# Interleaving the chunks of a seven-product FFN: the next chunk's first products among the last products of the chunk before, and three empty slots ahead of its third product

## The chip, the cores and the metric

One NeuronCore of a Trainium2 chip runs the whole program. The metric is device time in microseconds (us) of one execution. The kernel before was timed in three runs: 2363.18, 2362.95 and 2358.63 us, median 2362.95 us. One more execution, of 2361.89 us, was taken with the profiler; its instructions span 2360.2 us, and every duration in this document comes from it.

## The reference, cut to what matters

One layer on 256 tokens and 2048 channels, in float32:

```python
x = LN(ALPHA*x + 0.5*swiglu(x, ffn1_w1, ffn1_w3, ffn1_w2))
x = LN(ALPHA*x + mixer(x))          # mLSTM and stick-breaking branches
x = LN(ALPHA*x + 0.5*swiglu(x, ffn2_w1, ffn2_w3, ffn2_w2))
x = x + sigmoid(x @ w_ple_gate) * (p @ w_ple_proj)
swiglu(x, w1, w3, w2) = (silu(x @ w1) * (x @ w3)) @ w2   # 2048 -> 5632 -> 2048
```

The change touches only the two FFNs (the two swiglu calls). Their weights are 2048 x 5632 twice and 5632 x 2048, and each weight element is read at least once per FFN for just 256 tokens.

## The kernel before, in words

**Matmuls.** Each float32 operand is split in two float32r parts, hi and lo, and a product is made of three matmuls: hi x hi, hi x lo, lo x hi (L1046, L1047, L1048). The stationary operand is a 128 x 128 tile of the transposed activations `actT`, the moving one 128 x 512 of a weight. A **unit** is six such matmuls (256 rows of contraction) into one PSUM bank. The program is a Python list of units, and TensorE (PE) executes them in the order of this list.

**Weights.** A unit's weight is a `raw` tile of 256 x 512 (512 KB), loaded by a DMA issued on SP (L968). It is split by ScalarE (ACT, the cast at L995: hi) and VectorE (DVE, the subtraction at L999: lo). Splits are emitted in the order in which the units first use them, and the loop at L1008 to L1011 keeps seven of them alive, so that in an FFN a split is emitted seven or eight units ahead of its use. Loads run ahead of the splits: at most 12 raw tiles may be held in an FFN (`RAW_FFN`), and fewer where the 44 buffers of the `page` pool run short (L962, L963). ACT and DVE each execute in program order, so an instruction emitted behind a split waits until that split's raw tile has landed.

**FFN.** The 5632 hidden columns are 11 chunks of 512. Chunks 0 and 5 are computed plainly (`up`). The other nine (1, 2, 3, 4, 6, 7, 8, 9, 10) use `up7`: tokens in two halves, contraction in two halves, and the pair w1, w3 as two column blocks make a 2 x 2 block product that takes seven products instead of eight (function `seven`). Each product of a chunk is four units (a, b, c, d: one for each 512 rows of contraction). They go by the numbers in the code:

- product 1 uses a quarter t of w1; product 5 uses t plus a quarter of w3; product 6 uses that sum plus another quarter of w3; product 4 uses it plus the quarter b21 of w1, and product 2 b21 alone;
- products 7 and 3 use b12 + b22 and b22, loaded again from w3.

The two sums for products 5 and 6 are made in place by **growing** the raw tile: as soon as product 1's split has read t, a DMA issued on GpSimd (POOL, L328) adds the quarter of w3 to t in SBUF, and after product 5's split a second one adds the next. There are four tiles, so eight such DMAs for each chunk, 144 in all. The sums for products 4 and 7 are DVE additions (L333).

Products 1 and 2 accumulate in a bank X, 5 and 4 in a bank E. After 5d (the last unit of product 5) ACT copies E to SBUF (`e`, L443), and DVE writes X - e to a fixed bank B (L437); this write is called the **seed** below. Product 6 accumulates onto it, so 6a, product 6's first unit, cannot start before the seed. After 6d ACT copies B to the bank W (L448), onto which product 7 accumulates; product 3 goes on in B. After product 7 and 3 the two halves of the hidden chunk are finished (silu, multiplications at L459 and L470), transposed on PE (L264), copied by ACT (L266) and subtracted by DVE (L272) to make `actT` tiles for the down product.

**Order.** `weave` (L155) lays the list of the nine chunks' units (the side list) evenly among the other units of the FFN (the main list: chunks 0 and 5, and the down products `down(c)`, which need chunk c's hidden tiles). An entry `None` of the side list is an empty slot: it takes a place in the weaving and emits nothing. Before, the side list is the nine chunks one after another, each of 28 units and two empty slots between product 5 and product 6:

1a 1b 1c 1d | 5a 5b 5c 5d | two empty slots | 6a 6b 6c 6d | 2a 2b 4a 2c 4b 2d 4c 4d | 7a 3a 7b 3b 7c 3c 7d 3d

The 270 entries are woven among 184 main units. Between 5d and 6a then stand two main units (three in chunk 7), between 1a and 5a, counted from one to the other, six or seven units, and between 5a and 6a eight (nine in chunk 7).

Of the kernel before, what the change touches and what calls it, by code (L numbers as in the profile page):

```python
# [154 lines left out]
def weave(main, side):  # L155

    n = sum(isinstance(u, Unit) for u in main)
    out, at, seen = [], 0, 0
    for u in main:
        out.append(u)  # L160
        if isinstance(u, Unit):
            seen += 1
            while at < len(side) and at * n < seen * len(side):
                if side[at] is not None:
                    out.append(side[at])
                at += 1
    return out


def flat(pairs):  # L170
    return [u for p in pairs for u in p]
# [7 lines left out]
def kernel(  # L179
# [7 lines left out]
    x, out = x[0], out[0]  # L187
# [124 lines left out]
    def seven(wa, wb, rows, col0, cols, act, done):  # L312

        n = rows // (4 * P)
        banks = {k: {} for k in "XEBW"}

        def unit(m, i, tile, src, half, sub, bank, first):
            u = Unit(tile, half, banks[bank], src, i, sub, first and i == 0, i == n - 1,
                     lambda ps, t, m=m: done(m, banks))
            u.onto = not first  # L320
            return u
# [15 lines left out]
        one, five, six, two, four, rest = [], [], [], [], [], []  # L337
        for i in range(n):
# [8 lines left out]
            b12, b22 = quarter(wb, i, 0), quarter(wb, i, 2)  # L347
            rest.append(unit(7, i, Weight(b12, [b12, b22], [b12], plus(b12, b22)), act.forms, 1, 0, "W", False))
            rest.append(unit(3, i, Weight(b22, [], [b22]), act.forms, 1, 2, "B", False))
        lead = two[:1]  # L350
        for i in range(n):
            lead += two[i + 1:i + 2] + four[i:i + 1]
        return one + five + [None, None] + six + lead + rest

    program = []

# [53 lines left out]
    def ffn(w1, w3, w2, act, norm, skew=True, ahead=()):  # L410
        n = FF // COL
# [21 lines left out]
        def up7(c):  # L433
# [35 lines left out]
            def late(w):  # L469
# [4 lines left out]
                yield  # L474

            return seven(w1, w3, D, c * COL, COL, act, done)

        def down(*chunks):
            pairs = []
            for g in range(D // COL):  # L480
                def add(ps, t, g=g):
                    xs = xres[t][:, g * COL:(g + 1) * COL]
                    nc.vector.scalar_tensor_tensor(out=xs, in0=ps, scalar=0.5, in1=xs,  # L483
                                                   op0=ALU.mult, op1=ALU.add)
                    if n - 1 in chunks:
                        norm.chunk(t, g)
                pairs += group(w2, [c * COL + r for c in chunks for r in (0, 2 * P)], g * COL, COL, hT, add)
            return pairs
# [2 lines left out]
        program.extend((skewed(gate[0][:SKEW]) if skew else flat(gate[0][:SKEW])) + flat(gate[0][SKEW:]))  # L491
        rest, tail = down(8, 9), down(10)
        main = flat(hidden[0] + gate[1] + down(0) + down(1) + down(2) + down(3) + down(4) + hidden[1] + down(6) + down(5, 7))
        program.extend(main[:8] + weave(main[8:] + flat(rest[:8]), [u for c in (1, 2, 3, 4, 6, 7, 8, 9, 10) for u in up7(c)]))
        program.append(norm.load)
        program.extend(ahead)
        program.extend(flat(rest[8:]) + flat(tail[:-SKEW]) + skewed(tail[-SKEW:]))
# [12 lines left out]
    x1T = ActT(act_tile)  # L510
    norm1 = Norm(ln1_g[0], ln1_b[0], x1T, None)
    ffn(ffn1_w1[0], ffn1_w3[0], ffn1_w2[0], xT, norm1, skew=False, ahead=[lambda: mixer_setup()])


# [361 lines left out]
    x3T = ActT(act_tile)  # L876
    norm3 = Norm(ln3_g[0], ln3_b[0], x3T, None)
    ffn(ffn2_w1[0], ffn2_w3[0], ffn2_w2[0], x2T, norm3)


# [147 lines left out]
    for u in program:  # L1028
# [6 lines left out]
        j = u.tile.index  # L1035
# [50 lines left out]
```

## Time and profile before

| | |
|---|---|
| median of three runs | 2362.95 us (2358.63 to 2363.18) |
| the profiled execution | 2361.89 us, span 2360.2 us |
| first FFN, its woven part from chunk 2's product 6 to chunk 10's | 153.8 to 676.5 us |
| mixer and the plain products around it | about 771 to 1481 us |
| second FFN, the same woven part | 1626.3 to 2154.1 us |
| PE, PE weight loads, DVE, ACT, POOL busy in the whole span | 2236.6, 1839.7, 1734.9, 1260.3, 221.4 us |

How to read the views: PE is the engine that has the most work, so what counts is where PE waits and where its matmuls start further apart than they could. The view of the waits says who waited for whom (total us, times, longest). The timeline lists instructions in order of time (start, duration, engine, line, what it writes and reads, in brackets the idle time before it and what ended it); "x2" marks two instructions merged in one row. The view by windows gives busy time of each engine in a stretch, the granted PE clock as a share of full speed, the share of time in which the 16 DMA engines were busy, and the rate in GB/s.

### The profile page before, as it was taken

To read this page: it belongs to the slowest core of one execution; us is meant where nothing else is said; L and a number is where in the kernel's file an instruction comes from. 1 tells how busy PE (TensorE), PEld (TensorE's weight loads), DVE (VectorE), ACT (ScalarE), POOL (GpSimd) and SP (SyncE) were. 2 spreads that over 40 slices of the span, in tenths; PEclk is the share of its full clock that TensorE was granted. 3 is DMA by queue.
4 is the path that set the end of the run, shared out by engine and by line. 5 is a ranking of instruction groups with operands and counts; after the bars stand their busy time and mean duration, and the time that the engine had idled before them with its cause. 6 is when DMAs were issued, how large, how long until landed. Compare 5 with 4: busy or idle time off the path is not lost. (4 is left out here: it accounts for less than half of the span.)

```text
span 2360.2 us, 27588 instructions
## 1 busy us (share of the span) xinstructions
PE 2236.6 (95%) x10017; PEld 1839.7 (78%) x10017; DVE 1734.9 (74%) x1884; ACT 1260.3 (53%) x1471; POOL 221.4 (9%) x191
## 2 busy tenths in 40 slices
PE   9898998999989999999999999998899899998999
PEld 7676877788768888888888888777687777876878
DVE  6877898898878765654445556887789788886874
ACT  5555565665555455544643443555555556555542
POOL 3011101111000000100100000301111011100000
PEclk9899999999999999999999999999999999999999
DMA  9778988889785565665566577577897898978643
GB/s 322 212 193 244 268 245 235 232 221 290 223 262 209 172 187 160 177 182 158 161 188 196 182 228 248 147 226 199 226 271 242 233 240 204 289 221 254 242 149 108
DMA packets 267209, 510.22 MB, mean 216 GB/s; under 512 B 16000, under 2 KB 25024, under 8 KB 267072
## 3 DMA queue, kind: packets, MB, share of 16 engines
q1 hardware_dynamic: 227904, 432.95, 55.8%
q0 software_dynamic: 39168, 75.51, 18.0%
q8 instruction: 78, 1.28, 0.2%
q14 instruction: 59, 0.48, 0.1%
HBM read 506.30 MB, written 2.10 MB: 215 GB/s over the span
## 5 line engine op out<-in xcount | busy, mean ns | idle before, releaser
L999 DVE TENSOR_TENSOR split<-raw,split 128x1024 fp32r<-128x1024 f32 (+1 forms) x1037 | 1219.1, 1207 | 429.4 <-ACT split L995 406.7
L995 ACT CAST split<-raw 128x1024 fp32r<-128x1024 f32 (+1 forms) x1037 | 1042.2, 1037 | 659.2 <-DMA raw<-in_ffn_w_dram 250.2
L1046 PE MATMUL mm<-split,actT 128*128 128x512 f32 (+2 forms) x2704 | 1060.3, 392 | 15.2 <-ACT actT L258 12.8
L1048 PE MATMUL mm<-split,actT 128*128 128x512 f32 (+2 forms) x2704 | 1047.8, 387 | 8.8 <-DVE actT L272 7.5
L1047 PE MATMUL mm<-split,actT 128*128 128x512 f32 (+2 forms) x2704 | 1047.3, 387 | 4.7 <-DVE split L999 4.7
L1046 PEld LDWEIGHTS mm<-split,actT 128*128 128x128 f32 x2704 | 513.1, 190 | 118.7 <-ACT actT L258 15.0
L1048 PEld LDWEIGHTS mm<-split,actT 128*128 128x128 f32 x2704 | 512.4, 190 | 116.4 <-DVE actT L272 10.1
L1047 PEld LDWEIGHTS mm<-split,actT 128*128 128x128 f32 x2704 | 513.4, 190 | 106.0 <-DVE split L999 7.6
L328 POOL DMA_DIRECT2D raw<-in_ffn_w_dram x144 | 173.9, 1217 | 1105.4 <-DMA raw<-in_ffn_w_dram 589.7
L1046 PE MATMUL seeded<-split,actT 128*128 128x512 f32 x432 | 180.6, 418 | 84.2 <-DVE seeded L437 84.2
L1047 PE MATMUL seeded<-split,actT 128*128 128x512 f32 x432 | 177.6, 411 | 0.0
L1048 PE MATMUL seeded<-split,actT 128*128 128x512 f32 x432 | 176.6, 409 | 0.0
L333 DVE TENSOR_TENSOR raw<-raw 128x1024 f32<-128x1024 f32 x144 | 175.5, 1219 | 0.2 <-issue 0.2
L1046 PEld LDWEIGHTS seeded<-split,actT 128*128 128x128 f32 x432 | 86.5, 200 | 109.0 <-DVE seeded L437 91.0
L483 DVE SCALAR_TENSOR_TENSOR xres<-mm,xres 128x512 f32<-128x512 f32 x144 | 98.3, 685 | 7.0 <-PE mm L1048 7.0
L1048 PEld LDWEIGHTS seeded<-split,actT 128*128 128x128 f32 x432 | 86.9, 201 | 19.3
L1047 PEld LDWEIGHTS seeded<-split,actT 128*128 128x128 f32 x432 | 87.0, 201 | 17.8
L266 ACT CAST actT<-ms 128x512 fp32r<-128x512 f32 x84 | 48.9, 587 | 81.8 <-PE ms L264 79.3
L272 DVE TENSOR_TENSOR actT<-ms,actT 128x512 fp32r<-128x512 f32 x84 | 57.2, 685 | 22.2 <-ACT big L271 10.8
L407 POOL TENSOR_SCALAR xres<-xres 128x512 f32<-128x512 f32 x16 | 27.1, 1787 | 320.5 <-DVE xres L390 300.5
L236 ACT ACTIVATE temp<-mm 128x512 f32<-128x512 f32 (+1 forms) x36 | 20.5, 570 | 44.9 <-PE mm L1048 44.9
L236 ACT ACTIVATE big<-mm 128x512 f32<-128x512 f32 x20 | 12.0, 599 | 55.8 <-PE mm L1048 55.8
(124 smaller groups left out, 639.4 us busy)
## 6 DMA issues: line engine op xcount, KB each, us to landing
raw<-in_ffn_w_dram SPq DMA_DIRECT2D x527, 512.0 KB, 6.2
raw<-in_w_in_dram SPq DMA_DIRECT2D x168, 512.0 KB, 3.7
raw<-in_ffn_w_dram POOLq DMA_DIRECT2D x144, 512.0 KB, 9.6
raw<-in_w_out_dram SPq DMA_DIRECT2D x32, 512.0 KB, 5.1
raw<-in_w_ple_gate_dram SPq DMA_DIRECT2D x24, 512.0 KB, 4.9
raw<-in_w_up_m_dram SPq DMA_DIRECT2D x16, 512.0 KB, 3.7
raw<-in_w_up_sb_dram SPq DMA_DIRECT2D x16, 512.0 KB, 3.9
raw<-in_w_ple_gate_dram SPq DMA_DIRECT2D x16, 256.0 KB, 4.4
```

Source lines behind the costliest of these rows:

```text
L236: nc.scalar.activation(out, in_, func, **kw)
L266: nc.scalar.copy(dst[:, 0], ps[:])
L272: nc.vector.tensor_tensor(out=dst[:, 1], in0=ps[:], in1=dst[:, 0], op=ALU.subtract)
L328: nc.gpsimd.dma_start(out=raw.tile[:, :, :cols], in_=src.src, accum_op=ALU.add)
L333: nc.vector.tensor_tensor(out=a.tile[:, :, :cols], in0=a.tile[:, :, :cols], in1=b.tile[:, :, :cols], op=ALU.add)
L407: nc.gpsimd.tensor_scalar(out=xs, in0=xs, scalar1=ALPHA, scalar2=None, op0=ALU.mult)
L483: nc.vector.scalar_tensor_tensor(out=xs, in0=ps, scalar=0.5, in1=xs, op0=ALU.mult, op1=ALU.add)
L995: nc.scalar.copy(hi[:, ks], r[:, ks])
L999: nc.vector.tensor_tensor(out=lo[:, ks], in0=r[:, ks], in1=hi[:, ks], op=ALU.subtract)
L1046: nc.tensor.matmul(ps, hi, w[0][:, k, :u.cols], start=first, stop=False, skip_group_check=u.onto)
L1047: nc.tensor.matmul(ps, hi, w[1][:, k, :u.cols], start=False, stop=False, skip_group_check=u.onto)
L1048: nc.tensor.matmul(ps, lo, w[0][:, k, :u.cols], start=False, stop=last, skip_group_check=u.onto)
```

## The change

`seven` no longer joins its parts; a new function `chained` makes the side list of all nine chunks.

```diff
         rest.append(unit(3, i, Weight(b22, [], [b22]), act.forms, 1, 2, "B", False))
-        lead = two[:1]
-        for i in range(n):
-            lead += two[i + 1:i + 2] + four[i:i + 1]
-        return one + five + [None, None] + six + lead + rest
+        return one, five, six, two, four, rest
+
+    def chained(parts):
+
+        out = list(parts[0][0])
+        for j, (_, five, six, two, four, rest) in enumerate(parts):
+            ahead = list(parts[j + 1][0]) if j + 1 < len(parts) else []
+            n = len(five)
+            out += five + [None] * 3 + six + two[:1]
+            for i in range(n):
+                out += two[i + 1:i + 2] + four[i:i + 1] + (ahead[i - 2:i - 1] if i >= 2 else [])
+            ahead = ahead[n - 2:]
+            for i, u in enumerate(rest):
+                out += [u] + ahead[i:i + 1]
+        return out
...
-        program.extend(main[:8] + weave(main[8:] + flat(rest[:8]), [u for c in (1, 2, 3, 4, 6, 7, 8, 9, 10) for u in up7(c)]))
+        program.extend(main[:8] + weave(main[8:] + flat(rest[:8]), chained([up7(c) for c in (1, 2, 3, 4, 6, 7, 8, 9, 10)])))
```

The units are the same, and so are their loads, splits, growing DMAs and additions; their order is another. The four units of the next chunk's product 1 (written 1') stand behind 4c, 4d, 7a and 3a of the chunk before, and there are three empty slots in place of two:

5a 5b 5c 5d | three empty slots | 6a 6b 6c 6d | 2a 2b 4a 2c 4b 2d 4c 1'a 4d 1'b 7a 1'c 3a 1'd 7b 3b 7c 3c 7d 3d | 5'a ...

From 1a to 5a it is now 21 or 22 units (six, as before, in the first chunk, which has none ahead of it). The side list has 279 entries for the same 184 main units. Between 5d and 6a stand three main units, in chunks 2, 8 and 10 two; from 5a to 6a it is nine units, there eight. Line numbers from the middle of the file on rise by 11 (L443 is now L454, L995 is L1006).

The first place is ACT at the end of chunk 3 and the start of chunk 4 in the first FFN. Each row is an instruction; the raw tile that it reads tells the product. Before, chunk 4's four tiles t (raw_1973, raw_1998, raw_2018, raw_2020) are split for product 1 and shortly after for product 5:

```order
L995 CAST split_2115<-raw_1973 128x1024
L995 CAST split_2133<-raw_1985 128x1024
L995 CAST split_2146<-raw_1998 128x1024
L995 CAST split_2157<-raw_2018 128x1024
L995 CAST split_2169<-raw_2020 128x1024
L995 CAST split_2188<-raw_2033 128x1024
L995 CAST split_2201<-raw_1973 128x1024
L995 CAST split_2213<-raw_1998 128x1024
```

In the changed kernel the four tiles are raw_1712, raw_1846, raw_1922 and raw_1924. Their splits for product 1 stand among the splits of chunk 3's products 4, 7 and 3:

```order
L1006 CAST split_1939<-raw_1712 128x1024
L1006 CAST split_1951<-raw_1764 128x1024
L1006 CAST split_1964<-raw_1367 128x1024
L1006 CAST split_1979<-raw_1846 128x1024
L1006 CAST split_1998<-raw_1848 128x1024
L1006 CAST split_2012<-raw_1899 128x1024
L1006 CAST split_2025<-raw_1922 128x1024
L1006 CAST split_2039<-raw_1886 128x1024
L462 COPY temp_2058<-mm_1714 128x512
L236 ACTIVATE temp_1997<-mm_1457 128x512
L1006 CAST split_2061<-raw_1924 128x1024
```

Before, the first tile's next split (for product 5) came six rows on; now it comes 19 rows on, behind all of chunk 3's splits.

The second place is ACT around the copy `e` of chunk 4. Before, the copy (L443) stands behind the splits for 6a, 6b, 6c (raw_1973, raw_1998, raw_2018) and one main split, and ahead of 6d's (raw_2020):

```order
L995 CAST split_2294<-raw_1973 128x1024
L995 CAST split_2304<-raw_1998 128x1024
L995 CAST split_2315<-raw_2018 128x1024
L995 CAST split_2325<-raw_2063 128x1024
L443 COPY temp_2344<-mm_2287 128x512
L266 CAST actT_2352<-ms_2347 128x512
L995 CAST split_2355<-raw_2020 128x1024
```

Now, with the copy at L454, it reads:

```order
L1006 CAST split_2279<-raw_1712 128x1024
L236 ACTIVATE temp_2058<-temp_2058 128x512
L1006 CAST split_2297<-raw_1846 128x1024
L1006 CAST split_2308<-raw_1922 128x1024
L1006 CAST split_2318<-raw_2122 128x1024
L454 COPY temp_2330<-mm_2272 128x512
L1006 CAST split_2333<-raw_1924 128x1024
```

The same three splits of product 6 stand ahead of the copy; a silu of the chunk before (L236) has come between them. In chunks 2 and 8 it is four, 6d's split too, both in the changed kernel and before; in chunks 3 and 9 it was four and is three.

The third place is DVE around the seed of chunk 6, where the halves of chunk 4's hidden tile (actT) are made for `down(4)`. Before, the first half (actT_2843) and the last multiplication of the second (L470) stand well ahead of the seed (L437):

```order
L272 TENSOR_TENSOR actT_2843<-ms_2838,actT_2843 128x512
L470 SCALAR_TENSOR_TENSOR temp_2601<-seeded1_79,temp_2601 128x512
L999 TENSOR_TENSOR split_2855<-raw_2509,split_2854 128x1024
L999 TENSOR_TENSOR split_2866<-raw_2535,split_2865 128x1024
L999 TENSOR_TENSOR split_2876<-raw_2547,split_2875 128x1024
L999 TENSOR_TENSOR split_2886<-raw_2628,split_2885 128x1024
L483 SCALAR_TENSOR_TENSOR xres0_86<-mm_2831,xres0_86 128x512
L437 TENSOR_TENSOR seeded0_78<-mm_2764,temp_2902 128x512
L999 TENSOR_TENSOR split_2906<-raw_2567,split_2905 128x1024
L483 SCALAR_TENSOR_TENSOR xres1_87<-mm_2858,xres1_87 128x512
L272 TENSOR_TENSOR actT_2923<-ms_2918,actT_2923 128x512
```

Now they stand behind it (the seed is the first row, L481 the multiplication):

```order
L448 TENSOR_TENSOR seeded0_78<-mm_2590,temp_2895 128x512
L272 TENSOR_TENSOR actT_2903<-ms_2898,actT_2903 128x512
L481 SCALAR_TENSOR_TENSOR temp_2616<-seeded1_79,temp_2616 128x512
L1010 TENSOR_TENSOR split_2908<-raw_2462,split_2907 128x1024
L494 SCALAR_TENSOR_TENSOR xres1_87<-mm_2848,xres1_87 128x512
L1010 TENSOR_TENSOR split_2919<-raw_2694,split_2918 128x1024
L272 TENSOR_TENSOR actT_2934<-ms_2929,actT_2934 128x512
```

On PE, the first half's transposes stand directly behind 5d, one unit ahead of the first unit of `down(4)`, and the second half's directly ahead of the unit that needs them; before it was seven and two units between. Of chunk 9's halves, the second is now transposed one unit ahead of its use (before: eight).

## The prediction

> **What bounds the kernel now.** The page comes first, then the waits.
>
> ```profile
> PE 2236.6 (95%) x10017; PEld 1839.7 (78%) x10017; DVE 1734.9 (74%) x1884; ACT 1260.3 (53%) x1471; POOL 221.4 (9%) x191
> PE seeded L1046 <- DVE seeded L437: 84.2, 16, 8.9
> ACT split L995 <- DMA raw<-in_ffn_w_dram: 250.2, 132, 7.3
> ```
>
> PE is the bound, and of its idle time (2360.2 - 2236.6 = 124 us) the largest wait by far is 6a's wait for the seed: 84.2 us in 16 waits, one for each of chunks 2 to 10 in both FFNs (chunk 1 has none). The third row is a hint at its cause. Chunk 4's boundary in the timeline shows the chain:
>
> ```profile
> 292.98 1.20 POOL L328 DMA_DIRECT2D raw<-in_ffn_w_dram  x1 [1.97 <-DVE split L999]
> 297.70 0.40 PE L1048 MATMUL mm<-split,actT 128*128 128x512 f32 x1
> 302.03 1.99 ACT L995 CAST split<-raw 128x1024 fp32r<-128x1024 f32 x2 [1.54 <-DMA raw<-in_ffn_w_dram]
> 303.93 0.58 ACT L443 COPY temp<-mm 128x512 f32<-128x512 f32 x1
> 305.39 0.68 DVE L483 SCALAR_TENSOR_TENSOR xres<-mm,xres 128x512 f32<-128x512 f32 x1
> 305.99 0.69 DVE L437 TENSOR_TENSOR seeded<-mm,temp 128x512 f32<-128x512 f32 x1
> 306.73 0.80 PE L1046 MATMUL seeded<-split,actT 128*128 128x512 f32 x1 [5.45 <-DVE seeded L437]
> 310.25 0.40 PE L1048 MATMUL seeded<-split,actT 128*128 128x512 f32 x1
> 311.17 0.39 PE L1046 MATMUL mm<-split,actT 128*128 128x512 f32 x1
> 325.48 0.39 PE L1046 MATMUL mm<-split,actT 128*128 128x512 f32 x1
> ```
>
> 5d's last matmul ends at 298.1, so the copy (L443) could have run then. It ran at 303.93, because on ACT it stands behind 6c's split (302.03), and that waited for the second growing DMA of tile c, issued at 292.98 and landed 9.0 us later. Seed and 6a follow at once. After the wait PE is slow: from 306.73 to 310.25 nine matmuls start in 3.52 us. Undisturbed, 63 start from 311.17 to 325.48: 0.227 us each, 1.36 us a unit, and nine take 2.05 us. So the wait costs 5.45 + 1.5 us. Where does the late landing come from?
>
> ```profile
> raw<-in_ffn_w_dram POOLq DMA_DIRECT2D x8, 512.0 KB, 9.4
> DMA to landing us min/median/max: 6.0/9.6/15.7
> 274.00:306.00 32.00, 27.29 (x125) 22.24 (x123) 23.01 (x26) 16.49 (x19) 9.67 (x8) 0.96 1.01 211
> 310.00:345.00 35.00, 35.00 (x156) 28.95 (x155) 33.95 (x32) 21.62 (x23) 0.00 (x0) 1.00 0.84 292
> ```
>
> All eight growing DMAs of chunk 4 are issued and land in 274 to 306 us: 32 us at 211 GB/s, with the DMA engines busy throughout (share 1.01). From 310 to 345 none is in flight; plain loads run at 292 GB/s, and PE is never idle. In the first stretch each of the four tiles goes through split, growing, split, growing, split, so product 5's splits wait as well, and the second growings start late. This is what the change pulls apart.
>
> **What can be gained.** The woven parts, from chunk 2's 6a to chunk 10's:
>
> ```profile
> 153.80:676.50 522.70, 484.13 (x2098) 395.50 (x2098) 436.97 (x426) 297.56 (x319) 67.49 (x56) 0.96 0.86 242
> 1626.30:2154.10 527.80, 487.42 (x2098) 398.17 (x2098) 437.19 (x426) 297.44 (x318) 67.56 (x56) 0.96 0.86 239
> 153.84 0.80 PE L1046 MATMUL seeded<-split,actT 128*128 128x512 f32 x1 [5.47 <-DVE seeded L437]
> 1626.29 0.79 PE L1046 MATMUL seeded<-split,actT 128*128 128x512 f32 x1 [6.10 <-DVE seeded L437]
> ```
>
> Each holds 339 units, 2034 matmuls, and 16 groups of four transposes (64: together the 2098). At 0.227 us a matmul, and 0.45 us that a group adds (0.90 us between the starts of two matmuls 0.45 us apart otherwise, in the rows at 447 below), the floor is 462 + 7 = 469 us. Excess: 53.7 + 58.8 us; chunk 2's waits (5.5 and 6.1 us) lie just ahead of the windows: 124 us in all. By terms alone it is 84.2 us of waits and 16 x 1.5 us of slow matmuls, 108 us; the rest is product 5 waiting for its own splits, and small items. I take 120 us as what the change could remove.
>
> **Part by part.**
>
> *Product 1 moved into the chunk before.* It removes no work: same units, 144 growing DMAs, same loads. The first growings now start with 1a to 1d's splits, 21 units (29 us) ahead of 5a in place of 7 (9.5 us), against a landing time of at most 15.7 us in the row above: product 5's splits no longer wait, and the second growings find an emptier queue. I cost the first growings at nothing; the tail's 29 us hide them. Without that cover the present state returns.
>
> *What is late next* is the second growing, since 5a to 6a grows by only about one unit. Chunk 8 is the model, as there the first growings happened to land in time:
>
> ```profile
> 513.72 1.20 POOL L328 DMA_DIRECT2D raw<-in_ffn_w_dram  x1 [1.67 <-DVE split L999]
> 517.69 0.39 PE L1046 MATMUL mm<-split,actT 128*128 128x512 f32 x1
> 520.95 1.05 ACT L995 CAST split<-raw 128x1024 fp32r<-128x1024 f32 x1 [1.49 <-DMA raw<-in_ffn_w_dram]
> 521.91 0.57 ACT L443 COPY temp<-mm 128x512 f32<-128x512 f32 x1
> 523.93 0.50 PE L1046 MATMUL seeded<-split,actT 128*128 128x512 f32 x1 [1.52 <-DVE seeded L437]
> 1999.74 0.79 PE L1046 MATMUL seeded<-split,actT 128*128 128x512 f32 x1 [2.91 <-DVE seeded L437]
> ```
>
> Tile d's growing is issued 4.0 us ahead of 5d (517.69), lands after 7.2 us, and 6a waits 1.52 us (2.91 in the second FFN). Copy behind 6d's split and two units between: the changed kernel has this in chunks 2 and 8. I take 2.2 us, with 0.9 us of slow matmuls: 4 x 3.1 = 12 us. Elsewhere the copy stands behind 6c's split; tile c is issued one or two units earlier (1.4 to 2.7 us), and the third empty slot adds a unit (1.4 us), so 2.9 us less 2.8 to 4.1 leaves nothing: 0.5 us each for ten boundaries, 5 us. Chunk 10 has only two units between, and its growings are the slowest: 3 us each, 6 us. The landing time is the unknown: at 6 us all these terms vanish, at 12 us each boundary waits 2.5 us or more.
>
> How long a wait may be before matmuls slow down decides the 0.9 us:
>
> ```profile
> 447.24 0.39 PE L1048 MATMUL mm<-split,actT 128*128 128x512 f32 x1
> 447.47 0.60 PE L264 MATMUL ms<-ident,temp 128*128 128x128 f32 x4
> 448.14 0.39 PE L1047 MATMUL mm<-split,actT 128*128 128x512 f32 x1
> 453.35 0.68 PE L1046 MATMUL seeded<-split,actT 128*128 128x512 f32 x1 [2.53 <-DVE seeded L437]
> 457.10 0.40 PE L1046 MATMUL seeded<-split,actT 128*128 128x512 f32 x1
> ```
>
> After 2.53 us idle, nine matmuls took 3.75 us: 1.7 us lost. After the 1.52 us of chunk 8 the first matmul lasted 0.50 us in place of 0.80, the mark of a much shorter slow stretch. The Trainium skill ("TensorE: Matmul & The Clock Gate", Part 1) says that PE falls to half its clock after an idle window of about 3.4 us. By that, waits of 2 to 3 us would stay cheap, and the sum would be some 5 us lower; the row at 453.35 speaks against it, and the trace decides.
>
> *The turn of chunk 4.* `down(4)`'s two activation halves are now transposed one and no unit ahead of their use, directly behind 5d of chunk 6, with ACT's copies behind 6c's and 6d's splits and DVE's subtractions behind the seed:
>
> ```profile
> 519.05 0.60 PE L264 MATMUL ms<-ident,temp 128*128 128x128 f32 x4
> 522.38 0.58 ACT L266 CAST actT<-ms 128x512 fp32r<-128x512 f32 x1
> 523.78 0.68 DVE L272 TENSOR_TENSOR actT<-ms,actT 128x512 fp32r<-128x512 f32 x1
> ```
>
> Here a turn took 519.05 to 524.46, 5.4 us behind 6d's split and the copy; the bare operations are 1.9 us. With 1.4 us of cover for the first half and none for the second, the new waits are 2 to 6 us; I take 3 and 1 us of slow matmuls: 8 us in both FFNs. Chunk 9's second half, one unit of cover: 2 us.
>
> *Loads.* Four tiles t of the next chunk are now held during the tail, out of 12 raw tiles (8 where pages run short, ahead of chunk 10). Loads start later there; nothing to about 9 us per FFN (rival 3); I take 3 us for both.
>
> *Other queues.* DVE was busy 33.95 of 35 us in the old tail without delaying PE; spread over 44 us it has less to do per unit. POOL issues the same DMAs; that SP's loads pass four growings is rival 2. Extra empty slots cost nothing: main units fill them.
>
> **Sum:** 12 + 5 + 6 + 8 + 2 + 3 = 36 us remain of 120, a gain of 84. From the profiled 2361.9 us (the median is 1.1 us above it): **2278 us**, 3.5% faster.
>
> **Rivals.**
>
> 1. *The second growing still decides everywhere.* For it: four DMAs in a burst at 211 GB/s need 10 us, and 5a to 6a has hardly grown. Against it: chunk 8. If every boundary keeps 2.5 + 1.7 us, 67 us remain there and 13 elsewhere: 2322 us.
>
> 2. *The DMA engines become the bound of the tail.* The tail's loads (35 us at 292 GB/s, by the row at 310), 5 us for more main weights, and four growings (10 us at 211 GB/s) make 50 us of transfer in 44 us of PE. For: share 1.01 at 274. Against: from 310 to 345 the DMA engines had 16% to spare, and the tail's loads begin ahead of it. At 3 us per chunk: 2278 + 16 x 3 = 2326 us. The Trainium skill ("DMA: Bandwidth & Descriptors", Issuing engines are not separate DMA queues) says that transfers issued from SP and from GpSimd run on the same 16 engines and interleave. By this rule the first growings slow the tail's loads, as this rival has it; no row of before has a full stream of both, so the trace does not show by how much.
>
> 3. *Slower: too few free raw tiles.*
>
> ```profile
> raw<-in_ffn_w_dram SPq DMA_DIRECT2D x21, 512.0 KB, 6.6
> ```
>
> A load takes 6.6 us there (310 to 345), and a tail needs 24 of them in 44 us. With four in flight they take 24 x 6.6 / 4 = 40 us; with three, 53 us, 9 us late in each chunk: 2278 + 16 x 9 = 2422 us. It decides as soon as the held tiles leave three; 12 less four leaves more, eight less four does not leave many, so I expect it at most ahead of chunk 10.
>
> 4. *No effect:* the waits move from 6a to the units of `down` and of product 1 behind it, one for one: about 2362 us.
>
> **How the numbers follow.** Forecast (2250 to 2300): 0.60; rival 1: 0.17; rival 2: 0.12; rival 3: 0.07; rival 4: 0.04. With 108 to 124 us removable and 12 us remaining at best, 2250 is the low end; 2330 takes in rivals 1 and 2. Under 0.2% (4.7 us) a measurement of this kernel can't be told from no change. Faster: 0.89; within 0.2%: 0.04; slower: 0.07.
>
> **What would show it.** Right: 6a's 84 us down to some 25; the granted clock of the woven parts from 0.96 to 0.98 or more; ACT's wait for DMA well under 250 us; growings spread over the chunk; new waits of PE for L272 at `down(4)`. Wrong: waits of 2.5 us at every 6a (rival 1); PE waiting for splits in the tail with DMA share near 1 (rival 2), or with few loads in flight and DMA share below that (rival 3).

## The result, and the profile after

| | before | changed |
|---|---|---|
| median, same chip | 2361.41 us (2358.63 to 2363.18, 4 runs) | 2335.89 us (2332.00 to 2342.53, 4 runs) |
| profiled execution, span | 2361.89 us, 2360.2 us | 2336.99 us, 2335.2 us |
| ratio, 95% interval | | 0.9896 (0.9870 to 0.9922) |

The change makes the kernel faster by 25.5 us. The forecast was 84 us, and 2278 us; the measured time lies 6 us above the range's high end of 2330 us. The sign was right, the size was not.

The page of the changed kernel, and its waits. A row of the waits says who waited for whom: total us, times, longest.

```profile
PE 2229.2 (95%) x10017; PEld 1833.4 (79%) x10017; DVE 1730.4 (74%) x1884; ACT 1259.3 (54%) x1471; POOL 223.3 (10%) x191
PE seeded L1057 <- DVE seeded L448: 52.8, 12, 6.6
ACT split L1006 <- DMA raw<-in_ffn_w_dram: 164.9, 74, 6.2
DVE raw L333 <- DMA raw<-in_ffn_w_dram: 54.8, 20, 5.9
```

6a's wait for the seed fell from 84.2 to 52.8 us, not to 25. Four of its sixteen places are gone (chunks 6 and 7 in both FFNs), and the longest of the others is still 6.6 us. ACT waits 85 us less for DMA. New is the last row: DVE's additions (L333) wait 54.8 us for loads; before, they waited 0.2 us in all.

The two woven parts by windows, from chunk 2's 6a to chunk 10's (start:end, length, busy us of PE, PEld, DVE, ACT, POOL with their counts, granted clock, DMA share, GB/s):

```profile
147.90:663.30 515.40, 484.47 (x2098) 395.26 (x2098) 434.55 (x426) 295.87 (x317) 67.61 (x56) 0.97 0.86 243
1610.55:2128.85 518.30, 484.15 (x2098) 395.51 (x2098) 434.69 (x426) 296.60 (x318) 67.63 (x56) 0.97 0.86 243
```

With the same 2098 matmuls they are 7.3 and 9.5 us shorter (522.7 and 527.8 before); the rest of the gain lies ahead of chunk 2's 6a and behind chunk 10's. The clock rose by 0.01 only.

Chunk 4's boundary again, from the timeline, as in the prediction:

```profile
276.80 1.20 POOL L328 DMA_DIRECT2D raw<-in_ffn_w_dram  x1 [17.20 <-DVE split L1010]
279.07 2.44 POOL L328 DMA_DIRECT2D raw<-in_ffn_w_dram  x2 [1.07 <-DVE split L1010]
282.88 1.21 POOL L328 DMA_DIRECT2D raw<-in_ffn_w_dram  x1 [1.36 <-DVE xres L494]
284.94 1.05 ACT L1006 CAST split<-raw 128x1024 fp32r<-128x1024 f32 x1 [5.29 <-DMA raw<-in_ffn_w_dram]
288.02 0.60 PE L264 MATMUL ms<-ident,temp 128*128 128x128 f32 x4
288.96 1.05 ACT L1006 CAST split<-raw 128x1024 fp32r<-128x1024 f32 x1 [2.44 <-DMA raw<-in_ffn_w_dram]
292.79 1.99 ACT L1006 CAST split<-raw 128x1024 fp32r<-128x1024 f32 x2 [2.78 <-DMA raw<-in_ffn_w_dram]
294.69 0.58 ACT L454 COPY temp<-mm 128x512 f32<-128x512 f32 x1
296.08 1.04 ACT L1006 CAST split<-raw 128x1024 fp32r<-128x1024 f32 x1 [0.82 <-DMA raw<-in_ffn_w_dram]
296.14 0.69 DVE L448 TENSOR_TENSOR seeded<-mm,temp 128x512 f32<-128x512 f32 x1
296.89 0.80 PE L1057 MATMUL seeded<-split,actT 128*128 128x512 f32 x1 [5.52 <-DVE seeded L448]
297.03 0.58 ACT L266 CAST actT<-ms 128x512 fp32r<-128x512 f32 x1
298.90 0.68 DVE L272 TENSOR_TENSOR actT<-ms,actT 128x512 fp32r<-128x512 f32 x1
```

The four second growings now leave POOL between 276.80 and 282.88, all of them ahead of 5d (from 285.29 on). Still ACT waits 2.4 to 2.8 us ahead of one split after the other (288.96, 292.79), since the tiles land one after the other, and copy e stands behind the second of them. 5d's result is there at 286.8; the copy runs at 294.69. The turn whose transposes ran at 288.02 is copied only at 297.03, for the same reason. The first growings are out of this chain, and the end of the chain has hardly moved.

### The profile page after: what moved, and what is told of

Read it like the earlier page. It is cut to its first block, busy times and chain, and to the rows that moved or that the text cites. A ratio compares the mean times of both kernels' runs of the same rounds, so it can differ in the third digit from the quotient of the medians.

```text
span 2335.2 us, 27582 instructions
## 1 busy us (share of the span) xinstructions
PE 2229.2 (95%) x10017; PEld 1833.4 (79%) x10017; DVE 1730.4 (74%) x1884; ACT 1259.3 (54%) x1471; POOL 223.3 (10%) x191
## 4 chain that ended last, share of the span: by engine, by line
PE 52%; issue 15%; DMA 6%; DVE 3%; POOL 2%; ACT 0%; POOLq 0%; ACTq 0%; DVEq 0%
PE mm L1057 15%; PE mm L1059 15%; PE mm L1058 15%; DMA raw<-in_ffn_w_dram 5%; POOL raw L328 2%; PE seeded L1057 2%; PE seeded L1058 2%; PE seeded L1059 1%; PE ms L264 1%; DVE split L1010 1%; DVE xres L403 1%; DMA temp<-in_conv_m_dram 0%; DVE xres L401 0%; DVE xres L404 0%; ACT split L1006 0%
## 5 line engine op out<-in xcount | busy, mean ns | idle before, releaser
L1006 ACT CAST split<-raw 128x1024 fp32r<-128x1024 f32 (+1 forms) x1037 | 1038.1, 1037 | 619.1 <-DMA raw<-in_ffn_w_dram 164.9
L1059 PE MATMUL mm<-split,actT 128*128 128x512 f32 (+2 forms) x2704 | 1049.0, 388 | 12.3 <-DVE actT L272 11.5
L1057 PE MATMUL seeded<-split,actT 128*128 128x512 f32 x432 | 177.7, 411 | 52.8 <-DVE seeded L448 52.8
L333 DVE TENSOR_TENSOR raw<-raw 128x1024 f32<-128x1024 f32 x144 | 175.4, 1218 | 54.8 <-DMA raw<-in_ffn_w_dram 54.8
L1058 PE MATMUL seeded<-split,actT 128*128 128x512 f32 x432 | 175.3, 406 | 4.7 <-DVE split L1010 4.7
L1059 PE MATMUL seeded<-split,actT 128*128 128x512 f32 x432 | 173.9, 403 | 0.0
L1057 PEld LDWEIGHTS seeded<-split,actT 128*128 128x128 f32 x432 | 85.0, 197 | 75.2 <-DVE seeded L448 57.8
L1058 PEld LDWEIGHTS seeded<-split,actT 128*128 128x128 f32 x432 | 85.1, 197 | 24.2 <-DVE split L1010 7.3
L494 DVE SCALAR_TENSOR_TENSOR xres<-mm,xres 128x512 f32<-128x512 f32 x144 | 97.9, 683 | 6.5 <-PE mm L1059 6.5
L1059 PEld LDWEIGHTS seeded<-split,actT 128*128 128x128 f32 x432 | 84.8, 196 | 18.3
L272 DVE TENSOR_TENSOR actT<-ms,actT 128x512 fp32r<-128x512 f32 x84 | 57.1, 684 | 25.2 <-ACT actT L266 13.7
L236 ACT ACTIVATE temp<-mm 128x512 f32<-128x512 f32 (+1 forms) x36 | 20.7, 576 | 48.9 <-PE mm L1059 48.9
L236 ACT ACTIVATE big<-mm 128x512 f32<-128x512 f32 x20 | 12.0, 598 | 55.8 <-PE mm L1059 55.8
```

What stands on the lines that cost most here:

```text
L236: nc.scalar.activation(out, in_, func, **kw)
L272: nc.vector.tensor_tensor(out=dst[:, 1], in0=ps[:], in1=dst[:, 0], op=ALU.subtract)
L333: nc.vector.tensor_tensor(out=a.tile[:, :, :cols], in0=a.tile[:, :, :cols], in1=b.tile[:, :, :cols], op=ALU.add)
L1006: nc.scalar.copy(hi[:, ks], r[:, ks])
L1057: nc.tensor.matmul(ps, hi, w[0][:, k, :u.cols], start=first, stop=False, skip_group_check=u.onto)
L1058: nc.tensor.matmul(ps, hi, w[1][:, k, :u.cols], start=False, stop=False, skip_group_check=u.onto)
```

## The experiments

Two sums are read from PE's rows for every kernel below, over both FFNs but for their first nine units. A wait is the start of a unit less the start of the matmul before it, less 0.227 us; the time lost inside is what a unit's six starts take beyond 5 x 0.227 us (slow matmuls, a split or a turn that comes late inside the unit). Turns (L264 to L272) and late splits are waited for by units of main too. In us, wait + lost inside:

| kernel | time | 6a | main units | product 5 | products 3 and 7 | all units |
|---|---|---|---|---|---|---|
| before | 2361.9 | 87 + 17 | 20 + 14 | 17 + 13 | 1 + 0 | 178 |
| changed | 2337.0 | 55 + 13 | 25 + 27 | 13 + 4 | 1 + 6 | 154 |
| e1_slots | 2354.7 | 63 + 16 | 34 + 22 | 18 + 11 | 0 | 171 |
| e2_order | 2355.4 | 77 + 15 | 23 + 20 | 13 + 6 | 1 + 5 | 178 |
| e4_six | 2333.6 | 18 + 5 | 64 + 29 | 13 + 6 | 1 + 6 | 151 |
| e5_hold | 2302.2 | 0 + 6 | 44 + 21 | 3 + 3 | 1 + 21 | 119 |
| e6_hold_before | 2279.1 | 0 + 3 | 43 + 16 | 7 + 14 | 1 + 2 | 97 |
| e10_turn_before | 2262.2 | 0 + 5 | 19 + 11 | 15 + 17 | 1 + 3 | 82 |
| e12_half_first | 2251.5 | 0 + 6 | 32 + 17 | 0 | 1 + 0 | 69 |

The last column has all units, those of products 1, 2, 4 and 6b to 6d too. Times are those of the profiled execution for the first two rows, medians for the timed experiments, and a single execution for e12_half_first.

### The two parts of the change alone

e1_slots is the kernel before with three empty slots; e2_order is the changed order with two.

```diff
-        return one + five + [None, None] + six + lead + rest
+        return one + five + [None] * 3 + six + lead + rest
```

```diff
-            out += five + [None] * 3 + six + two[:1]
+            out += five + [None] * 2 + six + two[:1]
```

> Before's order of the units, with only the third empty slot between products 5 and 6. The slot puts about one more main unit (1.36 us) in front of each 6a. Theory A (the gain of 25.5 us comes from the interleaving, which takes the first growing out of the chain; the slot adds little): about 16 x 1.4 = 22 us at most if every wait shrinks by the whole unit, but since the chain split, growing, split, growing starts no earlier and product 5's splits are late themselves, I expect 8 to 15 us, 2346 to 2353 us. Theory B (the slot is most of the gain, the interleaving gives almost nothing): 2338 to 2342 us, 6a's waits from 84 down to some 60 us.

> The changed order with only two empty slots. Theory A (the interleaving carries the gain): 2336 us plus at most 16 x 0.7 = 11 us, 2340 to 2348 us; 6a's waits 60 to 75 us. Theory B (the slot carries it): 2355 to 2362 us, 6a's waits back to some 75 to 84 us.

Measured: e1_slots 2354.65 us, ratio 0.9982 (0.9972 to 0.9992), against 2359.44 us of before on that chip. e2_order 2355.44 us, ratio 0.9992 (0.9975 to 1.0010), no difference. Neither part alone is worth the 25 us, so neither theory accounts for the gain, though e2_order lies where theory B had it. Two rows of the waits of e1_slots, and one of e2_order's:

```profile
PE seeded L1046 <- DVE seeded L437: 60.6, 14, 6.2
PE mm L1046 <- ACT actT L266: 13.1, 2, 6.8
PE seeded L1057 <- DVE seeded L448: 74.7, 14, 8.4
```

In e1_slots 6a's loss (wait and loss inside) falls by 25 us and that of main units rises by 22; 13.1 us of this is a new wait of `down(4)`, once in each FFN, for ACT's copy of its turn. The wait moves from 6a to a unit of main near it. That was the prediction's rival 4, which it gave 0.04. In e2_order the waits move as well, but to more places: 6a and product 5 lose 11 and 10 us less, main units 9 us more, products 3 and 7 6 us, product 1 and 6b to 6d 3 us each.

### More distance

```diff
-            out += five + [None] * 3 + six + two[:1]
+            out += five + [None] * 6 + six + two[:1]
```

> The changed kernel with six empty slots in place of three between products 5 and 6: three to four more us between 5a and 6a. Theory A (the wait is a fixed distance: a second growing is issued about 2 us ahead of 5x and takes 7 to 14 us): 6a's 52.8 us shrink to under 15 us, with the slow matmuls behind them 45 to 55 us less, about 2285 to 2300 us, if the main units suffice. Theory B (what makes the growings late moves along: loads or the DMA engines bound the stretch, so the time goes to other waits of PE): 2322 us or more, with the waits at 6a replaced by waits for splits elsewhere.

Measured: 2333.58 us, ratio 0.9897 (0.9877 to 0.9916), as the changed kernel. 6a's wait fell from 55 to 18 us, and main's rose from 25 to 64, as theory B has it. The timeline of chunk 4's boundary there:

```profile
292.96 1.04 ACT L1006 CAST split<-raw 128x1024 fp32r<-128x1024 f32 x1 [2.68 <-DMA raw<-in_ffn_w_dram]
293.91 0.58 ACT L454 COPY temp<-mm 128x512 f32<-128x512 f32 x1
296.86 0.58 ACT L266 CAST actT<-ms 128x512 fp32r<-128x512 f32 x1
298.12 0.68 DVE L494 SCALAR_TENSOR_TENSOR xres<-mm,xres 128x512 f32<-128x512 f32 x1
298.86 0.79 PE L1057 MATMUL mm<-split,actT 128*128 128x512 f32 x1 [7.22 <-DVE xres L494]
```

PE now waits 7.22 us at a unit of main, whose bank DVE frees at L494, behind a subtraction that waits for product 6's split. Distance between 5d and 6a does not help, since splits are emitted seven or eight units ahead: product 6's splits, with their waits for growings, stand in ACT's and DVE's queues ahead of all that is due in those units. From this came theory Q (the queue).

### DVE's additions

e3_add_late emits each addition directly ahead of its own split; e7_no_add leaves the additions out.

```diff
-            make(j + 1)
-            if weights[min(j + 1, len(weights) - 1)].made or not weights[min(j + 1, len(weights) - 1)].make:
-                make(j + 2)
```

```diff
             def make():
-                nc.vector.tensor_tensor(out=a.tile[:, :, :cols], in0=a.tile[:, :, :cols], in1=b.tile[:, :, :cols],
-                                        op=ALU.add)
+                pass
```

> The changed kernel, with each addition of two weights (L333) put on DVE directly ahead of its own split and no longer one or two splits ahead, so that an addition that waits for a load holds back no earlier subtraction. Theory A (DVE falls behind in the tail because its additions wait 54.8 us for late loads in front of ready subtractions, so product 5's subtractions and with them the second growings come late): those waits no longer push the subtractions, 6a's waits fall from 52.8 to under 30 us, 2300 to 2320 us. Theory B (the loads themselves are late, or the growings land slowly beside loads, whatever DVE's order): 6a's waits stay at 45 to 60 us, 2330 to 2345 us.

> The changed kernel without DVE's additions L333 of two weights (it leaves out the sums t + w1's third quarter and w3's first + third quarters): 144 x 1.22 = 175 us of DVE work less, and no DVE wait of 54.8 us for late loads. Theory A (DVE's backlog after the tail makes the second growings late): 6a's waits from 52.8 to under 20 us, 2290 to 2310 us. Theories Q and L without a DVE backlog: growings are issued a little earlier at chunks 3, 4 and 9 only, 6a's waits 35 to 50 us, 2320 to 2335 us.

Measured: e3_add_late 2418.42 us, ratio 1.0256 (1.0238 to 1.0273). It told nothing of theory A, because it makes a wait of its own: ACT's cast now waits for an addition that stands behind the subtraction before it.

```profile
ACT split L1006 <- DVE raw L333: 398.2, 134, 5.0
```

In the changed kernel it was 84.9 us. e7_no_add took 2301.5 us in one run, 34 us less, with 6a's wait at 36.8 us: the time is theory A's, the wait that of Q and L. So DVE's additions and their waits for loads are a part of the loss, through second growings that are issued late, but with them gone two thirds of 6a's wait remain.

### The landing of the second growing

```diff
-        def grow(raw, src):
+        def grow(raw, src, ks=2):
...
-                nc.gpsimd.dma_start(out=raw.tile[:, :, :cols], in_=src.src, accum_op=ALU.add)
+                nc.gpsimd.dma_start(out=raw.tile[:, :ks, :cols], in_=src.src[:, :ks], accum_op=ALU.add)
...
-            w1.then, w5.then = grow(t, quarter(wb, i, 0)), grow(t, quarter(wb, i, 2))
+            w1.then, w5.then = grow(t, quarter(wb, i, 0)), grow(t, quarter(wb, i, 2), 1)
```

> The changed kernel with the second growing at half its size (256 KB in place of 512; it leaves out the second half of w3's third quarter in tile t). If the landing time of the second growings (7 to 14 us in a burst of four) sets 6a's wait, whether through ACT's queue (Q) or directly (L): landings of 4 to 7 us, 6a's waits under 15 us, 2280 to 2305 us. If their late issue behind DVE's subtractions sets it (A), with the landing a smaller part: 6a's waits 25 to 40 us, 2315 to 2330 us.

Measured: 2256.2 us in one run, 6a's waits 3.4 us: below the range of the first theory. The second growings land 6 to 7 us after their issue (medians by tile), in place of 8 to 12. What 6a waits for is the time that the second growings need; but half of them left out also takes traffic off the DMA engines everywhere, so not all of the 80 us need be 6a's.

### Product 6's splits held back

The hold lets no split of product 6 be emitted until product 5's last unit has been, so that copy e comes first in ACT's queue. `banks` gets its bank W where copy e is emitted.

```diff
             w1, w5, w6 = Weight(t, [t], []), Weight(t, [], []), Weight(t, [], [])
+            w6.held = banks
...
         while pos["split"] < most and len(splits) < limits(pos["split"])[1]:
+            b = getattr(weights[pos["split"]], "held", None)
+            if b is not None and "ps" not in b["W"]:
+                break
             split_one()
```

> The changed kernel, with product 6's splits held back until product 5's last unit has been written into the program, so that copy e, and a turn that is due there, stand ahead of them on ACT. Theory Q (ACT's queue: copy e and the turns wait behind 6's splits, which wait for growings; that alone costs the 55 us at 6a and most of the 42 us of stalls at units of main): 6a's waits below 15 us, main's stalls halved, 2285 to 2310 us. Theory L (the growings are simply late, whatever stands where): 6a to 6d then wait for their own splits by the same amounts, 2325 to 2345 us; as 6's splits are emitted 3 to 5 units later, other splits come late too and it may be slower than the changed kernel.

> The kernel before, with the same hold on product 6's splits and nothing else: order of units and two empty slots as before. Theory Q: the queue is a large part of before's 84 us too; copy e runs right behind 5d, so a part of the waits goes, but the chain split, growing, split, growing, split still ends late and 6a to 6d wait for their own splits: 2330 to 2350 us. Theory L: nothing gained, 2355 to 2365 us.

Measured: e5_hold (changed order) 2302.23 us, ratio 0.9774 (0.9744 to 0.9804). e6_hold_before (the order before) 2279.05 us, ratio 0.9671 (0.9647 to 0.9695). In both 6a's wait is gone, though the growings land as late as before (tile d, by medians, 8.8 us behind the start of 5d in e6_hold_before and 9.1 in before; 7.3 us in e5_hold and in the changed kernel): it was the copy's place on ACT that turned their lateness into PE's. Theory Q holds for 6a. Its other half misses: main's stalls were not halved, they rose from 52 to 65 us in e5_hold. For the kernel before the hold was worth far more than I expected (78 us below the 2357.21 us of before on that chip; expected were 10 to 30), as 6a to 6d hardly wait for their own splits (4 us for 6b to 6d). And with the queue right the changed order is **slower** than the old one, by 23 us.

What is left in e6_hold_before, at chunk 6's boundary:

```profile
348.54 0.59 ACT L444 COPY temp<-mm 128x512 f32<-128x512 f32 x1 [1.34 <-PE mm L1052]
349.74 0.60 PE L264 MATMUL ms<-ident,temp 128*128 128x128 f32 x4
351.05 1.05 ACT L996 CAST split<-raw 128x1024 fp32r<-128x1024 f32 x1 [0.97 <-DMA raw<-in_ffn_w_dram]
354.37 1.99 ACT L996 CAST split<-raw 128x1024 fp32r<-128x1024 f32 x2 [2.27 <-DMA raw<-in_ffn_w_dram]
358.38 1.04 ACT L996 CAST split<-raw 128x1024 fp32r<-128x1024 f32 x1 [2.02 <-DMA raw<-in_ffn_w_dram]
359.33 0.58 ACT L266 CAST actT<-ms 128x512 fp32r<-128x512 f32 x1
359.96 0.80 PE L1050 MATMUL mm<-split,actT 128*128 128x512 f32 x1 [6.79 <-ACT actT L266]
```

Copy e runs at once; the turn transposed 1.2 us later is copied 9 us after that, behind product 6's splits, and `down(4)` waits 6.79 us for it.

### The turns moved too

e10_turn_before is e6_hold_before with one delay changed, e11_turn_after is e5_hold with two; these put the turns' copies ahead of product 6's splits, or behind all four.

```diff
-    "after": 14.0, "form": 18.0, "ln_turn": 5.0, "ln_step": 1.7, "h": 8.0, "silu": 6.0, "late": 9.0, "rest": 1.2, "mt": 3.2,
+    "after": 14.0, "form": 18.0, "ln_turn": 5.0, "ln_step": 1.7, "h": 8.0, "silu": 6.0, "late": 7.0, "rest": 1.2, "mt": 3.2,
```

```diff
-    "after": 14.0, "form": 18.0, "ln_turn": 5.0, "ln_step": 1.7, "h": 8.0, "silu": 6.0, "late": 9.0, "rest": 1.2, "mt": 3.2,
+    "after": 14.0, "form": 18.0, "ln_turn": 5.0, "ln_step": 1.7, "h": 7.0, "silu": 6.0, "late": 12.0, "rest": 1.2, "mt": 3.2,
```

> The kernel before with the hold on product 6's splits, and the delay of the late multiplication 7.0 in place of 9.0, which puts the late turn's copies directly behind copy e, ahead of 6's splits on ACT. Theory Q (what stands behind 6's splits on ACT waits for the growings, a turn like the copy): the stalls of 6 to 7 us at down(4) and of 3 to 4 us at down(1) and down(8, 9) go, about 20 us of the 42 at units of main: 2258 to 2270 us. Rival (those units wait for something else, DVE's additions to the residual or the growings themselves): 2275 to 2285 us.

> The changed order with the hold, and the delays of the turns 7.0 and 12.0 in place of 8.0 and 9.0, which puts both turns of nearly every chunk before product 6's splits on ACT or behind all four. Theory Q: the stalls of 5 to 8 us at down(2) and down(4) go, about 25 us: 2270 to 2285 us, still 10 to 20 us above the other order with its turns moved, for the splits of products 3 and 7 that come late in the tail. Rival (the interleaving costs nothing by itself, its turns alone were badly placed): within 5 us of the other order with its turns moved.

Measured: e10_turn_before 2262.16 us, ratio 0.9585 (0.9565 to 0.9605): the fastest of all the complete kernels, 98 us below the kernel before on the same chip (2360.66 us), and main's waits from 43 to 19 us, as theory Q has it. Its granted clock is 0.993, before's 0.971. e11_turn_after 2297.47 us, ratio 0.9734 (0.9711 to 0.9757): a miss. The waits of 7.7 and 6.7 us at `down(2)` went, but at `down(4)` they grew from 5.7 and 4.9 to 9.4 and 10.8 us, because there a turn still stands behind product 6's splits. The late splits of products 3 and 7 remained (18 us lost inside their units, 21 in e5_hold).

### What the interleaving costs

In e5_hold the largest loss that e6_hold_before does not have is in the tail, at products 3 and 7: 21 us inside units, where e6_hold_before has 2. Chunk 9's tail in its timeline:

```profile
603.66 1.20 POOL L328 DMA_DIRECT2D raw<-in_ffn_w_dram  x1 [2.20 <-DVE split L1011]
607.89 1.23 DVE L333 TENSOR_TENSOR raw<-raw 128x1024 f32<-128x1024 f32 x1 [2.80 <-DMA raw<-in_ffn_w_dram]
610.55 1.20 POOL L328 DMA_DIRECT2D raw<-in_ffn_w_dram  x1 [5.69 <-DVE split L1011]
614.16 1.22 DVE L333 TENSOR_TENSOR raw<-raw 128x1024 f32<-128x1024 f32 x1 [2.18 <-DMA raw<-in_ffn_w_dram]
615.31 3.49 DVE L1011 TENSOR_TENSOR split<-raw,split 128x1024 fp32r<-128x1024 f32 x3
616.58 0.79 PE L1062 MATMUL seeded<-split,actT 128*128 128x512 f32 x1 [3.26 <-DVE split L1011]
```

DVE's additions wait for loads, the subtractions behind them come late, and PE waits 3.26 us inside 9.7b. The same stretch by windows:

```profile
588.00:620.00 32.00, 28.74 (x120) 23.27 (x119) 25.82 (x24) 16.67 (x18) 4.81 (x4) 0.93 1.02 292
```

There are four growings in it, and the DMA engines are busy throughout (share 1.02). Two causes could make the loads late: the growings' time on those engines (theory D, the prediction's rival 2), or the raw tiles that the four t hold (theory R, rival 3).

e12_half_first halves the first growing under the hold (with the `ks` of e9_half); e13_ten allows ten raw tiles in place of twelve under the hold; e14_half_first_alone halves the first growing in the changed kernel itself.

```diff
-            w1.then, w5.then = grow(t, quarter(wb, i, 0)), grow(t, quarter(wb, i, 2))
+            w1.then, w5.then = grow(t, quarter(wb, i, 0), 1), grow(t, quarter(wb, i, 2))
```

```diff
-RAW_FFN, RAW_MIX, RAW_EDGE = 12, 5, 4
+RAW_FFN, RAW_MIX, RAW_EDGE = 10, 5, 4
```

> The changed order with the hold, and the first growing at half its size (it leaves out the second half of w3's first quarter in tile t). Theory D (DMA engines: in the tail the first growings take the engines' time from the loads, so that additions and splits of products 7 and 3 come late): their late splits fall from 18 us to under 8, 2275 to 2288 us. Theory R (raw tiles: the four tiles t held through the tail leave fewer for loads ahead): nothing changes there, 2293 to 2303 us.

> The changed order with the hold, and ten raw tiles in place of twelve. Theory R: two free tiles less double the lateness in the tail, 2320 us or more, with 40 us or more of late splits at products 7 and 3. Theory D: the loads move the same bytes beside the same growings and are hardly later, 2298 to 2310 us.

> The changed kernel itself, without the hold, with the first growing at half its size (it leaves out the second half of w3's first quarter in tile t). It parts the 59 us that the change fell short by: the share that goes with the first growings' time on the DMA engines, beside tails' loads, is the difference to 2336 us. Theory D as a cause apart from ACT's queue: the loads come earlier, DVE's additions wait less, product 5's subtractions and second growings are issued earlier: 2295 to 2310 us, 6a's waits 25 to 40 us, DVE's 54.8 us of waits at L333 under 15. Theory Q alone (the queue behind 6's splits decides, the tail's loads matter only once that is gone): 2325 to 2336 us, 6a's waits 45 us or more.

Measured, one run each: e12_half_first 2251.5 us, 51 us less than e5_hold, more than theory D gave; the loss of products 3 and 7 fell from 21 us to none. e13_ten 2297.5 us, no slower than e5_hold: theory R falls. With ten tiles DVE's additions do wait longer for loads, 70.4 us in place of the 41.9 below, but products 3 and 7 lose no more (18 us). e14_half_first_alone 2288.2 us, 48 us less than the changed kernel and below the range. The additions' wait for loads, in the waits of e5_hold:

```profile
DVE raw L333 <- DMA raw<-in_ffn_w_dram: 41.9, 14, 5.9
```

of e12_half_first:

```profile
DVE raw L333 <- DMA raw<-in_ffn_w_dram: 7.3, 5, 2.4
```

and of e14_half_first_alone, where 6a still waits too:

```profile
DVE raw L333 <- DMA raw<-in_ffn_w_dram: 20.2, 14, 3.4
PE seeded L1057 <- DVE seeded L448: 30.8, 12, 4.7
```

So halving the first growings, at the place where the change puts them, is worth about 50 us with or without the hold, more than the hold is worth to the changed kernel (34 us). Theory D is borne out as a cause apart from the queue, but its size stays open: halving also takes 72 x 0.262 = 19 MB off the DMA engines altogether, and what it would be worth in the old order was not tried.

### Distance ahead of product 5

```diff
-        return one + five + [None, None] + six + lead + rest
+        return one + [None] * 2 + five + [None] * 2 + six + lead + rest
```

This is e10_turn_before with two empty slots more.

> The kernel before with the hold and the moved turns, and two empty slots between products 1 and 5 too (under one unit of main): the first growing has 1.1 us more. Theory (what is left is 5c's and 5d's wait for the first growing at chunks 3 and 10, 24 us in all there and at chunk 1): 5 to 10 us less than 2262 us. Rival: the unit is missing in the tail, whose splits come late by as much: 2258 to 2268 us, no difference that can be told.

Measured: 2267.91 us, ratio 0.9603 (0.9582 to 0.9623), against 0.9585 for e10_turn_before: nothing gained, as its rival has it; product 5's loss went from 32 to 27 us only, and main's rose from 30 to 42. The slots also moved a turn of four chunks ahead of copy e in ACT's queue, so this is no clean test of the distance.

## Why the prediction was right and wrong

**Right.** The sign; what bounds the kernel; that the first growings leave the chain (product 5's loss from 30 to 17 us, and what is left is all in chunk 1, whose product 1 was not moved); that the turns at `down(4)` become a new wait; and the chain itself, second growing, 6c's or 6d's split, copy e, seed, 6a. I quoted that chain, with the copy 5.8 us late on ACT, and then priced only its DMA end. The other end, the copy's place in the queue, was the one that could be had for nothing.

**Wrong, term by term.** The prediction let 36 us remain of 120. From PE's rows of the changed kernel, both FFNs: for 6a its wait, and what the nine starts behind it lose, as the prediction counts slow matmuls; for the turn wait and loss inside of its units:

| term | predicted | measured |
|---|---|---|
| 6a in chunks 2 and 8 | 12 | 9.1 + 2.1 = 11 |
| 6a in chunks 3, 4, 6, 7, 9 | 5 | 35.5 + 13.8 = 49 |
| 6a in chunk 10 | 6 | 10.4 + 3.6 = 14 |
| turn of chunk 4 at `down(4)` | 8 | 8.5 + 7.2 = 16 |
| chunk 9's second half | 2 | none found |
| loads late in the tail | 3 | 10 (late splits: 6 in products 3 and 7, 4 in main) |

That is 100 us in place of 36 us, and 44 of the 64 us between them are the second row; the first table's way of counting (154 less the 58 us that before had beyond its 120) gives 96.

The step that failed is **"What is late next"**, and there the taking of chunk 8 as the model for all boundaries: "7.2 us" to land, and "nothing" left over elsewhere. In chunk 8 of before the four second growings were issued over 8 to 10 us (over 8 to 13 us in chunks 2 to 10). When product 5 no longer waits, all four are issued within 5 to 8 us and line up for the DMA engines: the last lands 16 to 21 us after the first is issued. Medians over the 18 chunks, from POOL's and PE's rows:

| second growing of tile | a | b | c | d |
|---|---|---|---|---|
| before: issued ahead of its unit of product 5 | 4.2 | 3.2 | 2.1 | 1.0 |
| before: issue to landing | 10.8 | 10.0 | 9.4 | 9.2 |
| changed: issued ahead | 4.2 | 4.6 | 5.2 | 4.5 |
| changed: issue to landing | 7.9 | 9.5 | 11.7 | 12.4 |

Tile d is issued 3.5 us earlier against 5d, and takes 3.2 us longer; tile c 3.1 us earlier and 2.3 longer. So the landing against PE moves little: by medians tile d lands 7.3 us behind the start of 5d in place of 9.1. In chunks 3, 4 and 9 it lands later than before (10.5 to 11.5 us, before 7.1 to 9.6), and there 6a's wait is about as long as before. The prediction had the price for this case ("at 12 us each boundary waits 2.5 us or more") and rival 1, with the right mechanism (four DMAs in a burst), at 0.17; in chunks 3, 4 and 9 the waits are 5.4 to 6.8 us, more than its 2.5. In chunks 6 and 7 they are gone: there tile a's second growing is issued 4.9 to 6.4 us ahead of 5a, in 3, 4 and 9 only 0.7 to 2.6 us. In chunks 3 and 4 this goes with DVE's additions: in e7_no_add tile a's is issued 6.3 to 6.6 us ahead, and 6a's waits there fall from 22.5 to 9.9 us in all.

Rival 2 was real beside it, and it is the term that the sum put at nothing: "I cost the first growings at nothing; the tail's 29 us hide them". (The 3 us for loads are rival 3's.) They no longer delay product 5, but they delay the tail's loads. Their cost lies less in PE waiting in the tail (10 us) than in what DVE then does late: additions that wait 54.8 us for loads, and behind them product 5's subtractions and the second growings. "Spread over 44 us it has less to do per unit" counted DVE's work and not its waits. e7_no_add (34 us) and e14_half_first_alone (48 us) bear that out, in single runs that leave work out. Rival 3 fell (e13_ten). Rivals 1 and 2, at 2322 and 2326 us, came nearer to 2336 us than the forecast, each with a part of the cause.

Rival 4 is what the third slot shows when made alone, and in part the order. Why only the two together give 25 us is open in detail: which turns fall ahead of, among or behind product 6's splits differs from boundary to boundary, and that this decides it is not shown for every one.

## What to carry to other kernels

When a wait is traced to a transfer, look at what else stands in the waiting engine's queue behind the instruction that waits: letting independent work (here one copy and the turns) go first gained 98 us with the units in their old order, while moving the units, and their transfers with them, gained 25. Transfers taken off a chain arrive in a burst where the chain had spread them, so price the last of a burst, not one that was alone. And a wait that falls where it was aimed at is a gain only if the sum over all places of the engine falls with it.

## What the runs showed of the hardware

Accumulating DMAs cost the DMA engines almost twice as much for each MB as loads. The page of before says so in its part on queues (packets, MB, share of the 16 engines' span); the prediction did not read it:

```profile
q1 hardware_dynamic: 227904, 432.95, 55.8%
q0 software_dynamic: 39168, 75.51, 18.0%
```

q1 carries the loads, q0 the growings: 0.129% of the span for a MB against 0.238%, 1.85 times, or by the span of 2360.2 us 1.6 and 2.9 us of all 16 engines for 512 KB (0.524 MB). Read so, the new tail's four growings and 24 loads (the prediction's count) need 4 x 2.9 + 24 x 1.6 = 50 us in the 44 us that the prediction counted for it. That is the 50 us of its rival 2, which it had worked out from rates and then left out of the sum, since the old tail had 16% to spare. In the changed kernel the same stretch, 310 to 345 us, has a DMA share of 1.02 in place of 0.84.

Nor do the two run apart. By the profiles' pages, the median of the two FFNs' 527 full loads from issue to landing is 6.2 us in before, 7.9 us in the changed kernel, and 6.1 us in e14_half_first_alone, with the first growings halved, in this order:

```profile
raw<-in_ffn_w_dram SPq DMA_DIRECT2D x527, 512.0 KB, 6.2
raw<-in_ffn_w_dram SPq DMA_DIRECT2D x527, 512.0 KB, 7.9
raw<-in_ffn_w_dram SPq DMA_DIRECT2D x527, 512.0 KB, 6.1
```

The Trainium skill ("DMA: Bandwidth & Descriptors", Issuing engines are not separate DMA queues) says that transfers issued from different engines share the 16 DMA engines; by that rule the two slow each other, and the trace agrees with these numbers.
